# Stationary weight blocks laid out as element-wise mixed pairs and read with a step of two

## The chip, the cores and the metric

The kernel runs on one core of a Trainium2 chip. The metric is the device time of one execution in microseconds. Before the change the median of two timed runs is 977.47 us (976.68 and 978.26).

## What is computed

The reference is a two-layer decoder trunk for one sequence of 256 tokens and a model width of 1024, all in float32. Each layer has a feed-forward, a token mixer, and a second feed-forward; each of the three is preceded by an RMS norm that is shifted and scaled by vectors computed from a conditioning input `c`, and its result is added to the residual stream through a gate:

```
def swiglu(h, w_in, w_out):
    g, u = jnp.split(h @ w_in, 2, axis=-1)
    return (jax.nn.silu(g) * u) @ w_out

h = modulate(rms_norm(x, norm_g[layer, 0]), sh1, sc1)
x = x + 0.5 * g1[:, None, :] * swiglu(h, ffn_w_in[layer, 0], ffn_w_out[layer, 0])
h = modulate(rms_norm(x, norm_g[layer, 1]), sh2, sc2)
mix = diff_attention(...)        # layer 0; forgetting_attention(...) in layer 1
x = x + g2[:, None, :] * mix
h = modulate(rms_norm(x, norm_g[layer, 2]), sh3, sc3)
x = x + 0.5 * g3[:, None, :] * swiglu(h, ffn_w_in[layer, 1], ffn_w_out[layer, 1])
```

The hidden width of a feed-forward is 2816. The mixer of layer 0 is a differential attention of 8 heads, that of layer 1 a forgetting attention of 16 heads over one key and value pair that is computed once. Nearly all of the arithmetic is in products of the 256 tokens with weight matrices, and every weight is used once.

## The kernel before

**Precision.** A float32 product is made of three matmuls on operands in the type `fp32r`. A weight is split into a rounded high part `wh` (a copy on ScalarE) and a low part `wl` (raw minus high, on VectorE), and an activation likewise into `HH` and `HL` (or `hidh` and `hidl`). `mm3` then adds high times high, low times high and high times low into one bank of PSUM (line 405 on):

```
mm(ps, wh, xh, start=first, stop=False, skip_group_check=True)
mm(ps, wl, xh, start=False, stop=False, skip_group_check=True)
mm(ps, wh, xl, start=False, stop=last, skip_group_check=True)
```

The first operand of `mm` after the output is the stationary one: a block of 128 contraction rows (the partitions) by 128 output features, loaded into the array by a LDWEIGHTS; the second is the moving one, 256 tokens (258 where two columns with the shift vector ride along). A block is therefore loaded three times.

**The stream of weights.** All weights go through one stream in a fixed order (`stream`, line 230 on). An entry is a source in DRAM, its number of columns and a step, and it is cut into two or three pieces of at most 1024 columns (`pieces`). SyncE's queue fetches the pieces in order into `raw` tiles (six buffers), ScalarE makes `wh` (`cp_part`, six buffers) and VectorE makes `wl` (`sub_part`, five buffers) from each. `take` hands out the next entry and returns `blk(c, w)`, which gives the high and low views of the columns from `c` on, `w` wide:

```
def blk(c, w=P):
    o = c % step
    ...
    return his[p0 + c // step][:, o:o + w], los[p0 + c // step][:, o:o + w]
```

A product of weights by tokens asks for `w = 128`: the first feed-forward matrix (tiles `pf`, `pg` and `pu`, and `lg` and `lu` where it starts before the norm is known), the second (`po<-hidh` and `po<-hidl`, eleven blocks to an entry), the query and key projections (`lp`, `pqk`, `pk`, `lq`) and the output projections (`pw`). Where the output is wanted with tokens on the partitions, the weights are the moving operand: the value projections (`pv`, 512 columns) and the last feed-forward's second matrix (`po<-wh` and `po<-wl`, 256 columns, entries named `wlast`).

**Order of work.** The engines' programs are in the order in which the Python code issues instructions. A small planner (`InOrder`) keeps an estimated clock for each engine, with a cost that goes by the shape of an instruction's first operand (its output), and fills the gaps of ScalarE and VectorE with the splits of later pieces and with the blocks of the conditioning product (`ada_block`). `blk` also tells it when the first piece of an entry is done with.

**Layout.** `_layout` arranges every weight on the host as plain arrays, before the launch: `gu`, `kouter`, `bpairs`, and the lines for `wout` and `wqk` put the 128-column blocks that follow one another in use next to one another in memory.

Of the kernel before, what the change touches and what calls it, by code (L numbers as in the profile page):

```python
# [17 lines left out]
P = 128  # L18
D = 1024
S = 256  # L20
NC = D // P
HD = 64
AH = 8
# [80 lines left out]
def trunk(ctx, tc, a, out):  # L104
# [125 lines left out]
    stream = []  # L230
# [4 lines left out]
    def add_ffn(l, i):  # L235
        if (l, i) == (0, 0):
            stream.extend((a["win0"][k], K0 * 512, 1024) for k in range(NC))
        n = 2 * (NG - K0 if (l, i) == (0, 0) else NG)
        stream.extend((a["win"][win0_of(l, i) + u], 2048, 1024) for u in range(n))
        if (l, i) == (1, 1):  # L240
            for u in range(4):
                stream.extend((a["wlast"][u, :, c:c + n], n, step)
                              for c, n, step in ((0, 2048, 1024), (2048, 2048, 1024), (4096, 1536, 768)))
        else:
            stream.extend((a["wout"][(2 * l + i) * 16 + u], 11 * P, 768) for u in range(16))
# [11 lines left out]
    stream += [(a["wo"][u], 2048, 1024) for u in range(4, 8)]  # L257
    add_ffn(1, 1)

    pieces = [(src, c0, min(step, ncols - c0), c0 + step >= ncols)  # L260
              for src, ncols, step in stream for c0 in range(0, ncols, step)]

    shift = {}
    for (l, i), j in ((0, 0), K0), ((0, 1), 1), ((1, 0), 0), ((1, 1), 1):
# [7 lines left out]
    raws, his, los = [], [], []  # L272
# [20 lines left out]
    def cp_part():  # L293

        u = len(his)
        n = pieces[u][2]
        act.t = max(act.t, used[u - NHI] if u >= NHI else 0.0)
        raw = raws[u]
        if u >= len(pieces) - 6:
            gated[0](raw[:, :n])  # L300
        wh = wp.tile([P, WB], F32R, tag="wh", name="wh")[:, shift.get(u, 0):]
        act.plainly(lambda: act.copy(wh[:, :n], raw[:, :n]))
        his.append(wh)

    def sub_part():

        u = len(los)
        if u == len(his):
            return
        n = pieces[u][2]  # L310
        dve.t = max(dve.t, used[u - NLO] if u >= NLO else 0.0)
        wl = wp.tile([P, WB], F32R, tag="wl", name="wl", bufs=NLO)[:, shift.get(u, 0):]
        dve.plainly(lambda: dve.tensor_tensor(wl[:, :n], raws[u][:, :n], his[u][:, :n].bitcast(F32),
                                              op=ALU.subtract))
        los.append(wl)
        w_dma()
# [8 lines left out]
    def take(src, split=False):  # L325

        u = taken[0]
        assert stream[u][0].tensor.name.endswith(src), (stream[u][0].tensor.name, src)
        p0 = done[0] = begun[0]
        while len(used) < p0:  # L330
            used.append(pe.t)
        while len(his) < p0 + 2:
            cp_part()
        while len(los) < p0 + 2:
            sub_part()
        taken[0] += 1
        begun[0] += 2
        step = stream[u][2]

        def blk(c, w=P):  # L340
            o = c % step
            if c >= step and not split and done[0] == p0:
                done[0] = p0 + 1
                used.append(pe.t)
            return his[p0 + c // step][:, o:o + w], los[p0 + c // step][:, o:o + w]
        return blk

# [559 lines left out]
    for k in range(0, NC, 2):  # L907
# [3 lines left out]
        if k % 4:  # L911
            i = k // 4
# [461 lines left out]
def _constants():  # L1374
    idx = np.arange(383)
    rel = 255 - idx
    n = np.maximum(rel, 0)
    me = NB // 2
    nf = np.maximum(n, 1).astype(np.float32)
    large = me + (np.log(nf / np.float32(me)) / np.float32(math.log(128 / me)) * np.float32(NB - me)).astype(np.int32)  # L1380
    large = np.minimum(large, NB - 1)
    bucket = np.where(n < me, n, large)
    hot = np.zeros((NB, 383), np.float32)
    hot[bucket, idx] = 8.0
    umask = np.where(rel < 0, NEG, 0.0).astype(np.float32)
    q = np.arange(P)
    cmask = np.zeros((P, S), np.float32)
    cmask[:, P:] = np.where(q[:, None] >= q[None, :], 0.0, NEG)
    ub = np.full((P, S), 8.0, np.float32)
    ub[:, :P] = np.where(q[:, None] <= q[None, :], 8.0, 0.0)  # L1390
    return dict(hot=hot, umask=umask, cmask=cmask, ub=ub, ident=np.eye(P, dtype=np.float32))


def _layout(x, c, ada_w, ada_b, norm_g, ffn_w_in, ffn_w_out, a_w_qkv, a_w_o, a_lambda,
            a_subln_g, rel_bias, kv_ada_w, kv_ada_b, kv_norm_g, kv_w, fgate_w, fgate_b,
            b_w_q, b_w_o, final_g):
    cat = np.concatenate
    r = {}
    r["x"] = x[0].T.reshape(NC, P, S).transpose(1, 0, 2)
    r["c"] = c.reshape(1, D)  # L1400

    def cols(v):
        return v.reshape(-1, P).T

    def pairs(m):
        m = m.reshape(-1, P, D)
        return m

    ada, adab = [], []

    def unit(b0, b1, v0, v1):
        ada.append(cat([b0, b1], axis=1))
        adab.extend([v0, v1])

    def ada_sec(wT, bb, sec):
        return wT[sec * D:(sec + 1) * D].reshape(NC, P, D), bb[sec * D:(sec + 1) * D].reshape(NC, P)

    def mod_pair(wT, bb, s_sc, s_sh):
        w1, b1 = ada_sec(wT, bb, s_sc)
        w0, b0 = ada_sec(wT, bb, s_sh)  # L1420
        for j in range(NC):
            unit(w1[j], w0[j], b1[j], b0[j])

    for l in range(2):
        if l == 1:
            mod_pair(kv_ada_w.T, kv_ada_b, 1, 0)
        wT = ada_w[l].T
        for s in range(3):
            mod_pair(wT, ada_b[l], 3 * s + 1, 3 * s)
            w, b = ada_sec(wT, ada_b[l], 3 * s + 2)  # L1430
            for j in range(0, NC, 2):
                unit(w[j], w[j + 1], b[j], b[j + 1])
    r["ada"] = np.stack(ada)
    r["vecs"] = cat([cols(norm_g), cols(kv_norm_g), cols(final_g), cols(a_subln_g), np.stack(adab, axis=1)], axis=1)

    def gu(w):
        g = w[:, :FF].reshape(NC, P, NG, 256)
        u = w[:, FF:].reshape(NC, P, NG, 256)
        return cat([g, u], axis=3)

    win = []
    for l in range(2):
        for i in range(2):
            w = gu(ffn_w_in[l, i])
            if (l, i) == (0, 0):
                r["win0"] = w[:, :, :K0].reshape(NC, P, K0 * 512)
                w = w[:, :, K0:]
            n = w.shape[2]
            win.append(w.reshape(2, 4, P, n, 512).transpose(3, 0, 2, 1, 4).reshape(2 * n, P, 2048))
    r["win"] = cat(win, axis=0)  # L1450
    w = ffn_w_out.reshape(4, FF, D)
    r["wout"] = w[:3].reshape(3, 2, 11, P, NC, P).transpose(0, 4, 1, 3, 2, 5).reshape(48, P, 11 * P)
    r["wlast"] = w[3].reshape(22, P, 4, 256).transpose(2, 1, 0, 3).reshape(4, P, 22 * 256)
    r["fin"] = final_g.reshape(1, D)

    def vmat(w):
        return w.reshape(2, 4, P, 2, 512).transpose(3, 0, 2, 1, 4).reshape(4, P, 2048)

    def kouter(w):
        return w.reshape(4, 2, P, D).transpose(0, 2, 1, 3).reshape(4, P, 2048)  # L1460

    def bpairs(w):
        return w.reshape(NC, P, 4, 256).transpose(2, 1, 0, 3).reshape(4, P, 2048)

    w = a_w_qkv[0]
    qk = cat([w[:, :D].reshape(NC, P, AH, P), w[:, D:2 * D].reshape(NC, P, AH, P)], axis=3)
    r["wqk"] = qk.transpose(2, 1, 0, 3).reshape(AH, P, 2048)
    r["wv"] = vmat(w[:, 2 * D:])
    r["wo"] = cat([kouter(a_w_o[0]), kouter(b_w_o[0])], axis=0)
    r["wkk"] = bpairs(kv_w[:, :D])  # L1470
    r["wkv"] = vmat(kv_w[:, D:])
    r["wq"] = bpairs(b_w_q[0])
    r["fgw"] = fgate_w.reshape(NC, P, BH).transpose(1, 0, 2)
    r["fgb"] = fgate_b.reshape(BH, 1)
    k = _constants()

    def rows(v):
        return np.concatenate([v, np.zeros((P - v.shape[0], v.shape[1]), np.float32)], axis=0)

    r["misc"] = cat([k["ident"], k["cmask"], k["ub"], rows(k["hot"]),  # L1480
                     np.broadcast_to(k["umask"], (P, 383)), rows(rel_bias),
                     np.broadcast_to(a_lambda.reshape(1, 4 * HD), (P, 4 * HD))], axis=1)
    return {k: np.ascontiguousarray(v) for k, v in r.items()}
# [16 lines left out]
```

## Time and profile before

| | |
|---|---|
| median of two timed runs | 977.47 us |
| span of the profiled execution, first to last instruction | 974.4 us |
| TensorE matmuls | busy 963.7 us (99%), 8124 |
| TensorE weight loads | busy 939.9 us (96%), 8124 |
| VectorE | busy 818.5 us (84%) |
| ScalarE | busy 552.4 us (57%) |
| moved by DMA | 268.22 MB, mean 275 GB/s |

The page gives the span of the profiled execution and no separate total time for it. PE is the matmul side of TensorE and PEld its weight loads; DVE is VectorE, ACT ScalarE. Matmuls overlap one another in the records (each is listed with about 276 ns while one starts every 113 ns or so), so the listed durations of matmuls can't be added up; start times and counts within a stretch of the timeline can. L99 is the line of the helper that records nearly all instructions, so instructions are told apart by their tiles, written output<-inputs.

### The profile page before, as it was taken

To read this page: it belongs to the slowest core of one execution; us is meant where nothing else is said; L and a number is where in the kernel's file an instruction comes from. 1 tells how busy PE (TensorE), PEld (TensorE's weight loads), DVE (VectorE), ACT (ScalarE), POOL (GpSimd) and SP (SyncE) were. 2 spreads that over 40 slices of the span, in tenths; PEclk is the share of its full clock that TensorE was granted. 3 is DMA by queue.
4 is the path that set the end of the run, shared out by engine and by line. 5 is a ranking of instruction groups with operands and counts; after the bars stand their busy time and mean duration, and the time that the engine had idled before them with its cause. 6 is when DMAs were issued, how large, how long until landed. Compare 5 with 4: busy or idle time off the path is not lost.

```text
span 974.4 us, 20491 instructions
## 1 busy us (share of the span) xinstructions
PE 963.7 (99%) x8124; PEld 939.9 (96%) x8124; DVE 818.5 (84%) x1372; ACT 552.4 (57%) x902; POOL 54.6 (6%) x94
## 2 busy tenths in 40 slices
PE   8999999999999999999999999999999999999997
PEld 6999999998999999999997999999998999999997
DVE  7989979989999999878899989989977699555575
ACT  5466545566787645455576554445567576455432
POOL 0000200000112000000000000000011014300000
PEclk9999999999999999999999999999999999999999
DMA  9988999967776699888959899998885337978651
GB/s 360 415 352 279 332 372 339 345 225 272 293 239 232 209 381 370 293 287 314 329 179 370 308 338 337 345 314 319 297 278 174 104 109 228 266 149 276 185 152 44
DMA packets 69473, 268.22 MB, mean 275 GB/s; under 512 B 9417, under 2 KB 10225, under 8 KB 59266
## 3 DMA queue, kind: packets, MB, share of 16 engines
q1 hardware_dynamic: 66016, 259.69, 76.1%
q0 software_dynamic: 3072, 6.92, 2.5%
q8 instruction: 63, 1.03, 0.4%
q10 hardware_dynamic: 290, 0.32, 0.1%
q14 instruction: 32, 0.26, 0.1%
HBM read 264.75 MB, written 2.66 MB: 274 GB/s over the span
## 4 chain that ended last, share of the span: by engine, by line
PE 97%; DVE 1%; DMA 1%; ACT 0%; issue 0%; SPq 0%; DVEq 0%; ACTq 0%
PE po L99 25%; PE pg L99 21%; PE pu L99 21%; PE pf L99 5%; PE pv L99 5%; PE pw L99 4%; PE lp L99 4%; PE pqk L99 3%; PE wb L99 1%; PE lq L99 1%; PE lu L99 1%; PE lg L99 1%; PE pk L99 1%; PE sb L99 1%; DMA ada<-in_ada 1%; PE s L99 1%
## 5 line engine op out<-in xcount | busy, mean ns | idle before, releaser
L99 ACT CAST wh<-raw 128x1024 fp32r<-128x1024 f32 (+1 forms) x360 | 347.3, 975 | 210.8 <-PE pu L99 82.0
L99 DVE TENSOR_TENSOR wl<-raw,wh 128x1024 fp32r<-128x1024 f32 (+1 forms) x360 | 398.6, 1126 | 70.9 <-ACT sg L99 20.3
L99 DVE CUSTOM_DVE_ANT_0 ada<-ada,cact,vecs 128x1024 f32<-128x1024 f32 x160 | 203.6, 1279 | 0.4 <-DMA ada<-in_ada 0.4
L99 PE MATMUL pg<-HH,wh 128*128 128x256 f32 x608 | 168.0, 276 | 0.0
L99 PE MATMUL pg<-HH,wl 128*128 128x256 f32 x608 | 167.9, 276 | 0.0
L99 PE MATMUL pu<-HH,wh 128*128 128x256 f32 x608 | 167.9, 276 | 0.0
L99 PE MATMUL pu<-HL,wh 128*128 128x256 f32 x608 | 167.9, 276 | 0.0
L99 PE MATMUL pg<-HL,wh 128*128 128x256 f32 x608 | 167.9, 276 | 0.0
L99 PE MATMUL pu<-HH,wl 128*128 128x256 f32 x608 | 167.9, 276 | 0.0
L99 PE MATMUL po<-hidh,wh 128*128 128x256 f32 x528 | 145.7, 276 | 0.0
L99 PE MATMUL po<-hidh,wl 128*128 128x256 f32 x528 | 145.7, 276 | 0.0
L99 PE MATMUL po<-hidl,wh 128*128 128x256 f32 x528 | 145.7, 276 | 0.0
L99 PEld LDWEIGHTS pg<-HH,wh 128*128 128x128 f32 x608 | 114.1, 188 | 0.7 <-issue 0.6
L99 PEld LDWEIGHTS pg<-HH,wl 128*128 128x128 f32 x608 | 114.1, 188 | 0.0
L99 PEld LDWEIGHTS pu<-HH,wh 128*128 128x128 f32 x608 | 114.1, 188 | 0.0
L99 PEld LDWEIGHTS pg<-HL,wh 128*128 128x128 f32 x608 | 114.1, 188 | 0.0
L99 PEld LDWEIGHTS pu<-HL,wh 128*128 128x128 f32 x608 | 114.1, 188 | 0.0
L99 PEld LDWEIGHTS pu<-HH,wl 128*128 128x128 f32 x608 | 114.1, 188 | 0.0
L99 PEld LDWEIGHTS po<-hidh,wh 128*128 128x128 f32 x528 | 99.1, 188 | 0.0
L99 PEld LDWEIGHTS po<-hidl,wh 128*128 128x128 f32 x528 | 99.1, 188 | 0.0
L99 PEld LDWEIGHTS po<-hidh,wl 128*128 128x128 f32 x528 | 99.1, 188 | 0.0
L99 ACT CAST hidh<-hf 128x512 fp32r<-128x512 f32 x44 | 27.3, 621 | 40.5 <-DVE hf L99 40.4
(226 smaller groups left out, 1848.4 us busy)
## 6 DMA issues: line engine op xcount, KB each, us to landing
raw<-in_win SPq DMA_DIRECT2D x176, 512.0 KB, 6.8
ada<-in_ada SPq DMA_DIRECT2D x79, 1024.0 KB, 7.2
raw<-in_wout SPq DMA_DIRECT2D x48, 384.0 KB, 5.3
raw<-in_wout SPq DMA_DIRECT2D x48, 320.0 KB, 5.5
raw<-in_wqk SPq DMA_DIRECT2D x16, 512.0 KB, 5.8
raw<-in_wo SPq DMA_DIRECT2D x16, 512.0 KB, 5.8
raw<-in_wlast SPq DMA_DIRECT2D x16, 512.0 KB, 4.5
raw<-in_wv SPq DMA_DIRECT2D x8, 512.0 KB, 7.2
```

The source lines that it names most:

```text
L99: return self.tc.keep_in_program_order(f(*args, **kw))
```

## The change

The host writes the blocks of a pair (two neighbouring 128-column blocks, 256 columns) element by element in turn: first element of the first block, first element of the second, and so on (`mixed`). This is done for every weight that is used as a stationary operand. `blk`, asked for 128 columns, returns a view with a step of two elements that starts at the first or the second element of the pair. The pieces of `wout` hold eleven blocks to an entry, so that the last block of an entry has no partner; `mixed` leaves it as it is, and `blk` finds that the pair would reach past the piece (the fourth member of a stream entry gives a piece's width) and returns it as before. Views that are 256 or 512 wide are not touched.

```
+    stream = [(src, ncols, step, lambda i, n=ncols, s=step: min(s, n - i * s)) for src, ncols, step in stream]
     pieces = [(src, c0, min(step, ncols - c0), c0 + step >= ncols)
-              for src, ncols, step in stream for c0 in range(0, ncols, step)]
+              for src, ncols, step, _ in stream for c0 in range(0, ncols, step)]
...
+            if w == P:
+                o, n = o // 256 * 256, o // P % 2
+                if o + 256 <= stream[u][3](c // step):
+                    return tuple(t[p0 + c // step][:, o + n:o + 256:2] for t in (his, los))
+                o += n * P
             return his[p0 + c // step][:, o:o + w], los[p0 + c // step][:, o:o + w]
...
+    def mixed(w):
+        return np.swapaxes(w.reshape(w.shape[:-1] + (w.shape[-1] // 256, 2, P)), -1, -2).reshape(w.shape)
+
     def gu(w):
...
-        return cat([g, u], axis=3)
+        return mixed(cat([g, u], axis=3))
...
-    r["wout"] = w[:3].reshape(3, 2, 11, P, NC, P).transpose(0, 4, 1, 3, 2, 5).reshape(48, P, 11 * P)
+    w3 = w[:3].reshape(3, 2, 11, P, NC, P).transpose(0, 4, 1, 3, 2, 5).reshape(48, P, 11 * P)
+    r["wout"] = cat([mixed(w3[:, :, :10 * P]), w3[:, :, 10 * P:]], axis=2)
...
     def kouter(w):
-        return w.reshape(4, 2, P, D).transpose(0, 2, 1, 3).reshape(4, P, 2048)
+        return mixed(w.reshape(4, 2, P, D).transpose(0, 2, 1, 3).reshape(4, P, 2048))
...
     def bpairs(w):
-        return w.reshape(NC, P, 4, 256).transpose(2, 1, 0, 3).reshape(4, P, 2048)
+        return mixed(w.reshape(NC, P, 4, 256).transpose(2, 1, 0, 3).reshape(4, P, 2048))
...
-    r["wqk"] = qk.transpose(2, 1, 0, 3).reshape(AH, P, 2048)
+    r["wqk"] = mixed(qk.transpose(2, 1, 0, 3).reshape(AH, P, 2048))
```

## The prediction

> **What bounds the kernel now.** I read the page first: the share of each engine, the granted clock and the chain of work that ended last.
>
> ```profile
> span 974.4 us, 20491 instructions
> ...
> PE 963.7 (99%) x8124; PEld 939.9 (96%) x8124; DVE 818.5 (84%) x1372; ACT 552.4 (57%) x902; POOL 54.6 (6%) x94
> ...
> PEclk9999999999999999999999999999999999999999
> ...
> PE 97%; DVE 1%; DMA 1%; ACT 0%; issue 0%; SPq 0%; DVEq 0%; ACTq 0%
> ```
>
> TensorE is the bound in every stage: it carries 97% of the chain, and the granted clock is in its top step from the first slice to the last. Busy time says little for pipelined matmuls, so I went to start times. First the count per stretch (start:end, length, busy and number, clock, DMA share, GB/s), here 80 us inside the second feed-forward:
>
> ```profile
> 339.00:419.00 80.00, 80.00 (x708) 1.00 0.94 346
> ```
>
> Two of the 708 were already running when the stretch began, so 706 started in 80 us: one matmul each 113.3 ns. What makes up that interval is seen in the timeline of both TensorE queues (start, duration, engine, operation):
>
> ```profile
> 380.02 0.28 PE L99 MATMUL pg<-HL,wh 128*128 128x256 f32 x1
> 380.03 0.19 PEld L99 LDWEIGHTS pg<-HH,wh 128*128 128x128 f32 x1
> 380.14 0.28 PE L99 MATMUL pg<-HH,wh 128*128 128x256 f32 x1
> 380.14 0.19 PEld L99 LDWEIGHTS pg<-HH,wl 128*128 128x128 f32 x1
> ```
>
> A weight load starts at 380.03, about 0.01 us after the matmul before its own, and its matmul starts 0.11 us later, as the next load begins. So there is one load per matmul, and load and matmul fill the same 113 ns side by side. The change lengthens the kernel if the load becomes the slower of the two, and shortens it only if the load is what holds the matmul back now.
>
> How fast can contiguous loads follow each other? Where matmuls are short (128 columns of plain float32), the loads set the pace:
>
> ```profile
> 242.79 0.75 PEld L99 LDWEIGHTS po<-va,wt 128*128 128x128 f32 x6
> 243.46 0.19 PEld L99 LDWEIGHTS pqk<-HH,wh 128*128 128x128 f32 x1
> ```
>
> Six loads in 0.67 us are 111.7 ns each. Against 113.3 that leaves the load 1.6 ns of slack, 1.4%. That is the only cover the change has.
>
> And the moving side alone? The value projection streams 512 columns per load:
>
> ```profile
> 514.89 0.40 PE L99 MATMUL pv<-wh,HH 128*128 128x512 f32 x1
> ...
> 517.69 0.40 PE L99 MATMUL pv<-wh,HH 128*128 128x512 f32 x1
> ```
>
> Counting the rows between, twelve matmuls start in 2.80 us, 233.3 ns each. The second 256 columns come without a second load, and cost 233.3 - 113.3 = 120 ns, no less than the first. So I read the 113.3 ns as the pace of the moving stream, not as a cost of the load: a quicker load would find the matmul in its way.
>
> **The change part by part.** The host writes the weights in another order. The diff alters no size of a transfer, no tile, no number of instructions and no order: the planner's cost of a matmul goes by its output's shape, and the names it looks up are those of before. DMA, the two splits on ScalarE and VectorE, and every wait are as they were; they cost nothing more, and their cover (a TensorE that is the bound) stays unless TensorE itself gets faster. What changes is the read of the stationary block: 128 elements with a step of two, 8 bytes, spread over 1,024 bytes of a partition instead of 512.
>
> How many loads? The loads that read the low part, by tile (duration is min/median/max; the last number is the commonest form's count):
>
> ```profile
> L99 PEld LDWEIGHTS pg<-HH,wl x608: 187/188/191, 60.5 to 906.9; 128*128 128x128 f32 x152
> L99 PEld LDWEIGHTS pu<-HH,wl x608: 187/188/189, 61.3 to 907.5; 128*128 128x128 f32 x152
> L99 PEld LDWEIGHTS po<-hidh,wl x528: 187/188/188, 137.8 to 714.9; 128*128 128x128 f32 x176
> L99 PEld LDWEIGHTS po<-wl,hidh x176: 187/188/189, 907.9 to 967.5; 128*128 128x128 f32 x176
> L99 PEld LDWEIGHTS pf<-HH,wl x128: 186/188/192, 14.4 to 60.2; 128*128 128x128 f32 x128
> L99 PEld LDWEIGHTS lp<-HH,wl x96: 188/191/193, 197.6 to 726.9; 128*128 128x128 f32 x96
> L99 PEld LDWEIGHTS pqk<-HH,wl x96: 187/188/192, 234.1 to 277.6; 128*128 128x128 f32 x96
> L99 PEld LDWEIGHTS pv<-wl,HH x64: 187/188/192, 209.7 to 534.9; 128*128 128x128 f32 x64
> L99 PEld LDWEIGHTS pw<-oh,wl x64: 187/188/192, 277.9 to 306.1; 128*128 128x128 f32 x64
> L99 PEld LDWEIGHTS pw<-obh,wl x64: 187/188/192, 747.8 to 786.6; 128*128 128x128 f32 x64
> L99 PEld LDWEIGHTS lg<-HH,wl x32: 188/191/193, 306.4 to 797.9; 128*128 128x128 f32 x32
> L99 PEld LDWEIGHTS lu<-HH,wl x32: 189/190/192, 307.2 to 798.6; 128*128 128x128 f32 x32
> L99 PEld LDWEIGHTS pk<-HH,wl x32: 187/188/189, 499.3 to 509.8; 128*128 128x128 f32 x32
> L99 PEld LDWEIGHTS lq<-HH,wl x32: 187/191/193, 727.3 to 747.5; 128*128 128x128 f32 x32
> ```
>
> In two of these rows (po<-wl,hidh, the last down projection, and pv) the weights are the moving operand and stay contiguous. The other twelve sum to 608 + 608 + 528 + 128 + 96 + 96 + 64 + 64 + 4 x 32 = 2,320 blocks. mm3 loads each block three times (high, low, high): 6,960. Of the eleven blocks in half a column of the down projections the last has no partner and stays contiguous: 528/11 x 3 = 144. That leaves N = 6,816 loads with a step. Each nanosecond on the interval is 6.8 us, or 0.7% of the span; 2%, about what a measurement of this kernel can tell from no change, is 2.9 ns.
>
> The price of one stepped load is in no row, so I bound it. From below: the load keeps its 111.7 ns, hides behind the moving 113.3, and the sum is zero. Below zero: something in the pairing of load and matmul goes away. The shortest interval of a 128-column load that I find is in the transposes:
>
> ```profile
> 739.58 0.61 PE L99 MATMUL wa<-tri,d 128*128 128x128 f32 x4
> ...
> 740.02 0.38 PE L99 MATMUL wb<-tri,d 128*128 128x128 f32 x2
> ```
>
> Four in 0.44 us, 110 ns, or 109 within the rounding of the starts: (113.3 - 109) x 6,816 = 29 us less. From above, mildly: matmuls of the same shape (128 by 128 weights, 256 columns) run at other intervals elsewhere in this kernel, with contiguous loads.
>
> ```profile
> 53.73 0.28 PE L99 MATMUL pf<-HH,wh 128*128 128x256 f32 x1
> ...
> 54.79 0.28 PE L99 MATMUL pf<-HH,wh 128*128 128x256 f32 x1
> ```
>
> ```profile
> 510.40 0.28 PE L99 MATMUL pzf<-HH,fg 128*128 128x256 f32 x1
> ...
> 511.84 0.28 PE L99 MATMUL pzf<-HH,fg 128*128 128x256 f32 x1
> ```
>
> Nine matmuls in 1.06 us (117.8 ns), and twelve in 1.44 us (120 ns). From above, harshly: a stepped load at half rate, 2 x 111.7 = 223 ns.
>
> I take zero. The load delivers 128 elements in its 111.7 ns, 4 bytes each 0.87 ns; the moving stream takes 4 bytes each 0.44 ns from the same kind of memory. A load with a step of two passes over bytes at the moving stream's rate, 1,024 in about 113 ns, which that stream shows can be done. It is near the limit of 1.6 ns, though, and this is the weak point of the sum.
>
> The Trainium skill has a rule on just this (SBUF — State Buffer, section "Door 1: The DMA port swizzle", and Advanced Engine Details and Errata, "SBUF Cachelines"): lines are 16 bytes, and full bandwidth needs at least two hits on a line. A step of two float32 gives exactly two, so by the rule the load stays as it is and the sum is zero too; no run here shows a stepped load.
>
> The sum: 974.4 + 0 = 974.4 us of span. The page gives no other total for that execution; the median of the runs, 977.47, lies 3.1 us above the span, and I carry that over: 977.5 us. This case alone would land between 972 and 983.
>
> **The rivals.** *The stepped load is a little slower than the stream (slower).* If passing over twice the bytes costs the load a few per cent, its pace of 111.7 ns rises above the stream's, the load sets the interval, and matmuls wait for weights instead of for their own stream. It decides from 113.3 ns of load pace on, only 1.6 ns away; how far it goes I take from the intervals this kernel already shows, 117.8 to 120 ns. Priced by the two rows above: 4.5 x 6,816 = 31 us and 6.7 x 6,816 = 46 us, so 1,008 to 1,023 us. For it: in those rows loads and stream, both contiguous, already fall into a longer interval, and the step doubles the bytes that the load passes over. Against it: the feed-forward holds 113.3 over 706 matmuls beside full DMA traffic (share 0.94) and both splits.
>
> *The stepped load runs at half rate, or in between (much slower).* (223 - 113.3) x 6,816 = 748 us, 1,725 us. For it: nothing in the trace excludes it, since no load has a step. Against it: the moving stream's rate.
>
> *Load and stream stop disturbing each other (faster).* With the step both advance by the same bytes per time, and what separates 113.3 from 110 or 109 could go: 22 to 29 us, 948 to 955 us; if the load's 111.7 remains the floor, 1.6 x 6,816 = 11 us, 966 us, which is within 2%. Against it: the second 256 columns of pv cost 120 ns with no load beside them, and a gain of 4% meets a DMA share of 0.94 in the feed-forwards, so the last microseconds would turn into waits for weights.
> The Trainium skill (TensorE: Matmul & The Clock Gate, "Back-to-back issue gap") gives 262 cycles at 2.4 GHz for 256 columns, 109.2 ns, so 949 us if that were reached; the trace's 113.3 does not agree with it.
>
> *The change doesn't do what it says:* stepped reads could be turned into something else when the program is built. Then loads would change in number, which I fold into the harsh case.
>
> **How the numbers follow.** No change 0.41; mildly slower 0.27; harsh or in between 0.12; faster 0.20, of which a quarter stops at the load's floor. Beyond 2% faster (below 958): 0.15. Beyond 2% slower (above 997): 0.26 of the mild case and the 0.12, so 0.38. Within: 0.47. The range takes in 948 (the transposes' interval) and 1,030 (the mild case at 120 ns with a little more); left out are the harsh case and the edges, some 0.18.
>
> **What would show it.** Right: the feed-forward stretch again holds 113.3 ns per matmul, loads again start 0.01 us behind the matmul before, and the loads' forms keep their counts. The mild rival: the same stretch at 117 to 121 ns and the distance from load to matmul longer than 0.11 us, while pv and the last down projection, which keep contiguous reads, stay as they are. Faster: under 111 ns, and new idle time of TensorE on the high or low tiles. Wrong altogether: if stages without a stepped load moved, the cause is elsewhere.

## The result and the profile after

The changed kernel takes 1016.53 us (median of 1015.79 and 1017.28) against 977.47 us: 4.0% slower, ratio 1.0402 with a 95% interval from 1.0372 to 1.0432. The forecast case was "no change"; what came is the first rival of the prediction, a stepped load that is a little slower than the stream.

The page of the changed kernel, its lines on the span, the busy time, the granted clock and the chain of waits:

```profile
span 1013.7 us, 20491 instructions
...
PE 1003.9 (99%) x8124; PEld 981.3 (97%) x8124; DVE 821.9 (81%) x1372; ACT 554.5 (55%) x902; POOL 55.2 (5%) x94
...
PEclk9999999999999999999999999999999999999999
...
PE 97%; DVE 1%; DMA 1%; ACT 0%; issue 0%; SPq 0%; DVEq 0%; ACTq 0%
```

The span grew by 39.3 us and TensorE's busy time by 40.2 us. The number of instructions, the clock and the chain are those of before, and the work of the other engines nearly so: no wait was added, the matmuls themselves come at a longer interval. The count per stretch of the changed kernel, 80 us inside the second feed-forward (columns as in the prediction):

```profile
352.00:432.00 80.00, 80.00 (x669) 1.00 0.89 323
```

Two were already running, so 667 started in 80 us, one each 119.9 ns, where before 706 started. The timeline of both TensorE queues there:

```profile
352.19 0.28 PE L99 MATMUL pu<-HH,wl 128*128 128x256 f32 x1
352.19 0.20 PEld L99 LDWEIGHTS pu<-HL,wh 128*128 128x128 f32 x1
352.31 0.28 PE L99 MATMUL pu<-HL,wh 128*128 128x256 f32 x1
352.31 0.19 PEld L99 LDWEIGHTS pg<-HH,wh 128*128 128x128 f32 x1
```

The order is as before: a load starts with the matmul ahead of its own. But its matmul follows 0.12 us later instead of 0.11. The tiles of the changed kernel show which loads got longer (min/median/max in ns, first and last start in us):

```profile
L99 PEld LDWEIGHTS pg<-HH,wl x608: 193/193/199, 60.8 to 943.8; 128*128 128x128 f32 x152
...
L99 PEld LDWEIGHTS po<-hidh,wl x528: 187/193/199, 142.4 to 745.0; 128*128 128x128 f32 x176
...
L99 PEld LDWEIGHTS po<-wl,hidh x176: 187/188/189, 944.9 to 1006.8; 128*128 128x128 f32 x176
```

The stepped loads went from 187/188/191 to 193/193/199. The contiguous ones kept 187 to 189: those of the last down projection, and the eleventh blocks, which give `po<-hidh` its minimum of 187.

Where the time went, as the sum over all matmuls of a kind of the distance from one start to the next (worked out from the starts of both traces):

| tile | matmuls | before, us | after, us | gain in time |
|---|---|---|---|---|
| `pg`, `pu` | 3648 | 414.2 | 438.0 | 23.8 |
| `po`, down projections with stepped loads and small products | 1600 | 180.7 | 190.8 | 10.2 |
| `pqk`, `pw`, `pk` | 792 | 94.9 | 98.0 | 3.1 |
| `po`, last down projection, no stepped load | 528 | 59.9 | 62.1 | 2.2 |
| `pf`, `lp`, `lq`, `lg`, `lu`, all stepped | 960 | 117.9 | 117.7 | -0.2 |

These five rows hold 39.1 of the 39.3 us. Two of them fit neither the forecast nor the rival: a stage without a stepped load got slower, and a row of 960 stepped loads cost nothing in sum.

### The profile page after: what moved, and what is told of

Same layout as the page of the kernel before. It is cut to its first block, busy times and chain, and to the rows that moved or that the text cites. A ratio compares the mean times of both kernels' runs of the same rounds, so it can differ in the third digit from the quotient of the medians.

```text
span 1013.7 us, 20491 instructions
## 1 busy us (share of the span) xinstructions
PE 1003.9 (99%) x8124; PEld 981.3 (97%) x8124; DVE 821.9 (81%) x1372; ACT 554.5 (55%) x902; POOL 55.2 (5%) x94
## 4 chain that ended last, share of the span: by engine, by line
PE 97%; DVE 1%; DMA 1%; ACT 0%; issue 0%; SPq 0%; DVEq 0%; ACTq 0%
PE po L99 25%; PE pg L99 22%; PE pu L99 22%; PE pf L99 5%; PE pw L99 4%; PE pv L99 4%; PE pqk L99 3%; PE lp L99 3%; PE wb L99 1%; PE lq L99 1%; PE lg L99 1%; PE lu L99 1%; PE pk L99 1%; PE sb L99 1%; DMA ada<-in_ada 1%; PE s L99 1%
## 5 line engine op out<-in xcount | busy, mean ns | idle before, releaser
L99 PE MATMUL pu<-HH,wl 128*128 128x256 f32 x608 | 171.9, 283 | 0.0
L99 PE MATMUL pg<-HH,wl 128*128 128x256 f32 x608 | 171.9, 283 | 0.0
L99 PEld LDWEIGHTS pg<-HH,wh 128*128 128x128 f32 x608 | 118.1, 194 | 0.7 <-issue 0.6
L99 PEld LDWEIGHTS pg<-HL,wh 128*128 128x128 f32 x608 | 118.2, 194 | 0.0
L99 PEld LDWEIGHTS pu<-HL,wh 128*128 128x128 f32 x608 | 118.2, 194 | 0.0
L99 PEld LDWEIGHTS pu<-HH,wh 128*128 128x128 f32 x608 | 118.1, 194 | 0.0
L99 PEld LDWEIGHTS pg<-HH,wl 128*128 128x128 f32 x608 | 117.7, 194 | 0.0
L99 PEld LDWEIGHTS pu<-HH,wl 128*128 128x128 f32 x608 | 117.7, 194 | 0.0
L99 PEld LDWEIGHTS po<-hidl,wh 128*128 128x128 f32 x528 | 102.7, 195 | 0.0
L99 PE MATMUL po<-wl,hidh 128*128 128x256 f32 x176 | 49.5, 281 | 0.0
```

The costliest lines, as they stand in the source:

```text
L99: return self.tc.keep_in_program_order(f(*args, **kw))
```

## The experiments

Two theories stood after the result. *Slow load*: the stepped load by itself takes longer than the stream that covers it. *Interplay*: load and stream go together differently, and the load's own pace says little. All runs but one (e11) start from the kernel before, so their memory holds contiguous blocks and a step reads other columns. Without changes, the kernel before ran in 976.85, 981.17 and 981.24 us beside the three groups of runs (e1 to e4, e5 to e8, e9 to e11). These differ by more than some of the effects, so the argument goes by intervals of a stage, not by totals.

### e1: other loads stepped, the weights contiguous

```
-                        ts = slice(t * P, t * P + P)
+                        ts = slice(t, 2 * P, 2)
...
-                o = (k % 2) * 256 + t * P
+                o = slice((k % 2) * 256 + t, (k % 2) * 256 + 256, 2)
...
-            mm(po[:, 0:P], wt[:, 0:P], v0, start=True, stop=True)
-            mm(po[:, P:2 * P], wt[:, P:2 * P], v0, start=True, stop=False)
+            mm(po[:, 0:P], wt[:, 0:2 * P:2], v0, start=True, stop=True)
+            mm(po[:, P:2 * P], wt[:, 1:2 * P:2], v0, start=True, stop=False)
...
-            st[c] = [w0[:, j * P:j * P + P] for j in range(4)] + [w1[:, j * P:j * P + P] for j in range(2)]
+            st[c] = [w[:, b + j:b + 256:2] for w, b in ((w0, 0), (w0, 256), (w1, 0)) for j in range(2)]
```

> The kernel before, with the weight blocks contiguous; instead the loads that the change left alone are stepped by two: the token blocks in the value projections (pv, 512 moving columns) and in the last down projection (po<-wh, po<-wl, 256 moving columns), and the softmax blocks in the attention products (po<-va,wt with 128 and wb<-vb with 64 moving columns of plain float32). The tokens or keys of a block are then others than the product calls for; all work is done. Theory 'slow load': the stepped load itself takes longer whatever moves beside it. Then the light products go from 111.7 to about 118 ns a load, pv stays at 226 to 233 ns (the load ends long before the stream), po<-wh goes from 113.3 to 120. Rival 'contention': the load alone is as quick as before, and load and stream hinder each other while both read. Then the light products stay at 112, pv gets some 7 ns longer (236 to 240), po<-wh goes to 120. Both give some 981 us in all (528 x 6.7 ns = 3.5 us).

The best place to see a load by itself is `wb`, where a load goes with a matmul of only 64 columns, so that the loads set the pace. The timeline of the weight loads, first of the kernel before, then of e1:

```profile
743.59 0.97 PEld L99 LDWEIGHTS wb<-vb,wta 128*128 128x128 f32 x8 [0.33 <-issue]
744.48 0.53 PEld L99 LDWEIGHTS wb<-vb,wtb 128*128 128x128 f32 x4
```

```profile
745.83 1.02 PEld L99 LDWEIGHTS wb<-vb,wta 128*128 128x128 f32 x8 [0.33 <-issue]
746.77 0.55 PEld L99 LDWEIGHTS wb<-vb,wtb 128*128 128x128 f32 x4
```

Eight loads take 0.89 us contiguous and 0.94 us stepped: 111.3 and 117.5 ns each. And the last down projection, whose stationary token blocks are stepped in e1 (count per stretch, 915 to 960 us), first before and then in e1:

```profile
915.00:960.00 45.00, 45.00 (x399) 1.00 0.44 129
```

```profile
915.00:960.00 45.00, 45.00 (x377) 1.00 0.48 139
```

Less the two that were already running, 397 starts in 45 us are 113.3 ns and 375 are 120.0 ns. The prediction's stretch from 339 to 419 us, contiguous here, holds 113.3 ns as before (709 matmuls). `pv`, whose loads were stepped too, went from means of 229.0 and 230.6 ns in its two stages to 233.3 ns in both (by the starts of the traces): 3 to 4 ns more, which neither theory had (no change, or 236 to 240 ns). A load of about 118 ns ends long before a stream of 230, so this is a first sign that the load's own pace isn't the whole. So the step makes a load about 6 ns slower with other operands too, and this without any change in the layout of the weights.

### e2 and e9: steps of four and of three

```
+            if w == P:
+                p = p0 + c // step
+                b = min(o // (P * 4) * P * 4, pieces[p][2] - P * 4)
+                return tuple(t[p][:, b + o // P % 4:b + P * 4:4] for t in (his, los))
             return his[p0 + c // step][:, o:o + w], los[p0 + c // step][:, o:o + w]
```

(e9 has 3 in place of 4.)

> The kernel before, with the 128-column weight blocks read with a step of four elements (16 bytes), without the other layout, so the products use other columns than they call for; all work is done. It gives the law of the cost. If the step costs one fixed amount: 120 ns a matmul, about 1024 us. If it goes by the bytes passed over (6.7 ns for each 512 more, as from step one to two): 133 ns, 977 + 6960 x 20 ns = 1116 us. If each line of memory now serves one element and its reading time shows: a load of 213 ns or more and a matmul each 220 ns, 977 + 6960 x 107 ns = 1720 us. 'Slow load' and 'contention' do not differ here.

> The kernel before, with the weight blocks read with a step of three elements (other columns than called for; all work is done). With a step of four the interval was 233 ns, and 128 loaded elements then lie on 128 lines of 16 bytes: 1.82 ns a line. With a step of two they lie on 64 lines, 1.82 x 64 = 117 ns, near the 118 to 119 ns pace that was measured; contiguous on 32, 58 ns, so that the elements and not the lines set the 113. Theory 'a line each 1.82 ns': three elements of step touch 96 lines, 175 ns: an interval of 175 to 180 ns and 977 + 6960 x 62 to 67 ns = 1408 to 1443 us. Rival 'two hits or none' (a line with fewer than two elements costs a full access for each element): as with a step of four, 233 ns, about 1810 us.

Measured: 1810.08 us with a step of four and 1392.37 us with three. The timeline of matmuls in a feed-forward, e2 and then e9:

```profile
699.66 0.40 PE L99 MATMUL pu<-HL,wh 128*128 128x256 f32 x1
...
700.83 0.40 PE L99 MATMUL pg<-HH,wl 128*128 128x256 f32 x1
```

```profile
499.79 0.34 PE L99 MATMUL pu<-HH,wh 128*128 128x256 f32 x1
...
500.66 0.34 PE L99 MATMUL pu<-HL,wh 128*128 128x256 f32 x1
```

Both times five intervals lie between the two rows: 234 and 174 ns each. Counted in 16-byte lines (the width comes from the Trainium skill, SBUF — State Buffer, section "Door 1: The DMA port swizzle"), a load of 128 float32 touches 32 lines with step one, 64 with two, 96 with three and 128 with four. 174 / 96 = 1.81 ns and 234 / 128 = 1.83 ns: beyond step two the load costs about 1.82 ns for each line. In the last down projection, contiguous in both runs, the interval was 113.3 ns.

The 233 ns that e9's rival "two hits or none" expected of a step of three did not come, but that rival was worked out too roughly. With a step of three, every four elements lie on three lines, so 32 of the 96 lines hold two of them and 64 hold one. Take for a line of two what it costs at a step of two (118.9 / 64 = 1.86 ns, from e8 below) and for a line of one what it costs at a step of four (1.83 ns): 32 x 1.86 + 64 x 1.83 = 177 ns, near the 174 measured. So a line costs about the same whether one or two elements are taken from it, and that a line with a single hit is costly was not refuted. Nor do these runs tell lines from bytes: for steps of one to four the lines touched are the bytes passed over divided by 16, and 174 ns for 1,536 bytes and 234 ns for 2,048 are equally well 0.11 ns a byte. A step of more than four would separate the two; it was not run. The total of e9 lies below the 1408 to 1443 us expected, in part because the interval is 174 ns and not 175 to 180.

### e7 and e8: shorter streams, loads contiguous or stepped

```
-        mm(ps, wl, xh, start=False, stop=False, skip_group_check=True)
-        mm(ps, wh, xl, start=False, stop=last, skip_group_check=True)
+        mm(ps[:, :192], wl, xh[:, :192], start=False, stop=False, skip_group_check=True)
+        pe.t += (ps.shape[1] - 192) / 2350
+        mm(ps[:, :192], wh, xl[:, :192], start=False, stop=last, skip_group_check=True)
+        pe.t += (ps.shape[1] - 192) / 2350
```

(The line on `pe.t` keeps the planner's clock, and so the order, as it was. e8 also has e2's edit with 2 in place of 4.)

> The kernel before, contiguous, but the second and third matmul of each three stream 192 tokens instead of 256 (the low and cross terms of the last 64 tokens are left out). It gives the contiguous load's own pace beside the weights' type: if that is the 111.7 ns seen with short plain products, two of three intervals are 111 to 112 and the first 113, and the time is 977 - 4640 x 1.6 ns = 970 us. If the stream of 256 held everything and a load can be quicker still, below 965.

> As e7 (192 tokens in the second and third matmul of each three), with all weight blocks read with a step of two (other columns than called for). Theory 'slow load': the stepped load has a pace of about 118 ns of its own, which no shorter stream lowers: 117 to 119 ns in two of three, 1005 to 1012 us. Rival 'disturbed read': the 120 ns come from load and stream together, so that a stream a quarter shorter takes some of it away: 113 ns or below in two of three, 985 us or below.

Two of three streams are a quarter shorter, so the loads should show their own pace. The timeline of weight loads, e7 and then e8:

```profile
339.86 0.19 PEld L99 LDWEIGHTS pg<-HH,wl 128*128 128x128 f32 x1
...
340.88 0.19 PEld L99 LDWEIGHTS pg<-HH,wl 128*128 128x128 f32 x1
```

```profile
351.91 0.20 PEld L99 LDWEIGHTS pg<-HH,wh 128*128 128x128 f32 x1
...
352.98 0.20 PEld L99 LDWEIGHTS pg<-HH,wh 128*128 128x128 f32 x1
```

Nine intervals each: 1.02 us / 9 = 113.3 ns contiguous, 1.07 us / 9 = 118.9 ns stepped. Totals 972.74 and 1009.21 us. So a contiguous load of this kind has a pace of its own of 113.3 ns, not 111.7, and a stepped one 118.9 ns, 1.86 ns for each of its 64 lines. (The few us that e7 gained are no sign of 111.7: its feed-forwards stayed at 113.3 ns, while `lp`, which had 258 columns, went from 120.8 to 114.3 ns by the starts.) Of the 6.7 ns by which the interval grew in the changed kernel, the load's own pace would account for 5.6; e3 below shows that the load's pace isn't the whole of it.

### e4 and e6: shorter loads, contiguous or stepped

```
-        mm(ps, wl, xh, start=False, stop=False, skip_group_check=True)
-        mm(ps, wh, xl, start=False, stop=last, skip_group_check=True)
+        mm(ps[:64], wl[:, :64], xh, start=False, stop=False, skip_group_check=True)
+        mm(ps[:64], wh[:, :64], xl, start=False, stop=last, skip_group_check=True)
```

(In e6 these two loads take every second of a block's 128 columns, 64 in all; the first of the three stays contiguous. The low products of the other 64 output features are left out in both.)

> The kernel before, contiguous, but the second and third matmul of each three load 64 weight columns instead of 128 (the low and cross terms of the upper 64 features of a block are left out). The moving stream keeps its 256 columns. If the 113.3 ns are the pace of the stream, as the prediction read them: 113.3 ns stay and the time is 974 to 980 us. If the load of 128 columns holds the matmul back now: the two of three fall to 110 or below, 4640 x 3.5 ns = 16 us less or more, 961 us or below.

> As e4 (the second and third load of each three with 64 columns, the upper 64 features without their low and cross terms), but these 64-column loads are read with a step of two from a span of 128 columns (other columns than the product calls for); the first load is whole and contiguous. Theory 'slow load': what costs is the length of the stepped load; at 64 columns it is far shorter than the stream, so the intervals are those of e4, 113.3 or 117.8 by stage, and the time is 977 to 1005 us (e4: 988). Rival 'disturbed read': a stepped load hinders the stream whatever its length; then 120 ns everywhere, 1014 us or more.

The count per stretch in three stages, e4 and then e6:

```profile
160.00:190.00 30.00, 30.00 (x267) 1.00 0.93 340
345.00:385.00 40.00, 40.00 (x342) 1.00 0.97 376
560.00:600.00 40.00, 40.00 (x356) 1.00 0.94 345
```

```profile
160.00:190.00 30.00, 30.00 (x262) 1.00 0.92 330
345.00:385.00 40.00, 40.00 (x349) 1.00 1.00 390
560.00:600.00 40.00, 40.00 (x349) 1.00 0.92 333
```

Less two each, e4 has 113.2, 117.6 and 113.0 ns; by the starts of the trace these are stages at exactly 113.3 and 117.8 ns, held without a break over the stretches shown. Shorter loads never gave less than 113.3: the stream has that pace too. They even made whole stages slower, without any step, and the run took 988.08 us, which neither case had expected. e6 has 115.4, 115.3 and 115.3 ns (115.6 by the starts) in all three, and 987.57 us, which lies in the range given for 'slow load', but not by the intervals that it expected. A load of 64 elements with a step of two touches 32 lines, so at 1.82 ns for a line it would take 58 ns (an estimate from e2 and e9) and should not count at all. The load's pace alone does not explain either run.

### e3, e5 and e10: one stepped load in three, in 24, in six

e3, the low part alone:

```
+            if w == P:
+                p = p0 + c // step
+                b = min(o // 256 * 256, pieces[p][2] - 256)
+                return his[p][:, o:o + w], los[p][:, b + o // P % 2:b + 256:2]
```

e5, the low part of the first block of a piece (e10: of the first block of every pair):

```
+            if w == P and o == 0:
+                return his[p0 + c // step][:, o:o + w], los[p0 + c // step][:, 0:256:2]
```

> The kernel before, with only the low part's loads stepped by two (one load in three), without the other layout, so the low parts are those of other columns; all work is done. If the cost belongs to each stepped load: 2320 x 6.7 ns = 15.5 us, about 993 us, with 120 ns before the wl matmul and 113.3 before the two others. If it is a state into which the pair of load and stream falls and in which it stays: all three near 118 to 120, above 1005 us.

> The kernel before, with a step of two in one load of 24: the low part of the first block of each piece (320 loads); that low part is of other columns, all work is done. So far one stepped load in three made all three intervals 120 ns. Theory 'state': load and stream hold one of a few fixed intervals (113.3, 117.8, 120 ns) over whole stages, and a stepped load throws them out of the shortest; if they stay out, the whole feed-forwards run at 117.8 to 120 and the time is above 1000 us. Rival 'relaxation': a few matmuls after the stepped load the 113.3 is back; then the cost is 320 x 6.7 to 20 ns = 2 to 6 us, 979 to 984 us.

> The kernel before, with a step of two in the low part's load of every second block (one load in six, 1160 loads; other columns, all work is done). One in 24 cost some 20 ns for each stepped load, spread over the four matmuls behind it; one in three and three in three both ended at 120 ns. Theory 'each stepped load costs 20 ns until the matmuls behind it are all at 120': 20/6 = 3.4 ns on the mean, 116.7 ns, and 1160 x 20 ns = 23 us, about 1000 us. Rival 'a jump between one in 24 and one in three': the pair doesn't recover between, 119 to 120 ns and about 1015 us.

Measured: 1016.03, 981.88 and 995.14 us. The count per stretch in the second feed-forward, e3, e5 and e10:

```profile
352.00:432.00 80.00, 80.00 (x669) 1.00 0.88 323
```

```profile
339.00:419.00 80.00, 80.00 (x703) 1.00 0.93 343
```

```profile
352.00:432.00 80.00, 80.00 (x688) 1.00 0.89 329
```

e3 has the very count of the changed kernel, with a third of its stepped loads. What one of them costs: the starts are 667, 701 and 686, and at 113.3 ns they would fill 75.59, 79.45 and 77.75 us. The rest of the 80 us, shared among 667/3, 701/24 and 686/6 stepped loads, is about 20, 19 and 20 ns each (in e5 one start more or less in the stretch would move this by 4 ns). The starts of e5 show how, around one stepped load:

```profile
341.79 0.28 PE L99 MATMUL pg<-HH,wh 128*128 128x256 f32 x1
341.90 0.28 PE L99 MATMUL pg<-HH,wl 128*128 128x256 f32 x1
...
342.38 0.28 PE L99 MATMUL pg<-HL,wh 128*128 128x256 f32 x1
```

From the first row to the last are five intervals; to the nanosecond, in the trace, they are 115, 120, 122, 115 and 115, and then 113.3 again. They sum to 20 ns over five times 113.3. So a stray stepped load costs 20 ns, spread over the next few matmuls; at one in three the interval reaches 120.0 ns, and with all three stepped it stays there. That the longer interval lasts once it is entered fell with e5; that it relaxes within a few matmuls held, though one load cost 20 ns and not 6.7.

### e11: the changed kernel with a contiguous tail

```
-            if w == P:
+            if w == P and u < len(stream) - 13:
```

(In the changed kernel; the weights ahead of the last down projection still lie mixed, so the columns come in another order.)

> The changed kernel, with contiguous reads in the last piece pair (48 matmuls) of the last first-matrix, just ahead of the last down projection (the layout stays mixed, so these blocks are of other columns; all work is done). In the changed kernel the last down projection, which has no stepped load, ran at 117.8 ns instead of 113.3. If that is a state handed on from the stepped matmuls ahead: contiguous matmuls between let the pair fall back to 113.3, and the last down projection takes 59.9 us instead of 62.2, some 1013.5 us in all. If it comes of something else in the changed kernel: 117.8 stays.

The last down projection, 955 to 1000 us, in the changed kernel and then in e11:

```profile
955.00:1000.00 45.00, 45.00 (x384) 1.00 0.41 118
```

```profile
955.00:1000.00 45.00, 45.00 (x400) 1.00 0.40 118
```

382 starts are 117.8 ns, 398 are 113.1 (113.3 by the starts of the trace). The same instructions run at the one or the other pace, depending on what ran before them: with contiguous loads just ahead the stage is back at 113.3 ns. By the starts of e11, the 48 matmuls with contiguous reads of mixed blocks were themselves back at 113.3 ns a few matmuls after the last stepped load, so the order in memory costs nothing by itself. But stepped loads ahead do not always leave a longer interval. In the changed kernel and in e3 the last down projection follows a stage at 120.0 ns and stands at 117.8; in e2, e8 and e9 it follows stepped loads just as directly and stands at 113.3. The run took 1013.24 us, near the 1013.5 expected; single runs of one kernel differ by as much as the 2.2 us of this stage, so it is the interval that shows the effect and not the total.

## Why the prediction was wrong at its centre and right in its range

The measured 1016.53 us lie in the stated range, 948 to 1,030, because the range took in the mild rival, which had a chance of 0.27. The forecast itself, no change at 977.5 us, was 39 us too low.

*TensorE is the bound, nothing else moves.* Right. The chain holds 97% PE in both, and instructions, transfers and their order are the same.

*One load per matmul, side by side; the change lengthens the kernel if the load becomes the slower.* Right as a condition, and it is what happened; that the interval follows the load's pace alone is more than the runs show (see what stays open).

*"Against 113.3 that leaves the load 1.6 ns of slack."* Wrong. The 111.7 ns were read from `po<-va,wt`, plain float32 blocks beside short streams; in e7 the loads of weights run at 113.3 ns as soon as the stream is shorter. The slack was nil. *"So I read the 113.3 ns as the pace of the moving stream, not as a cost of the load"* was half right: e4 shows the stream's pace at 113.3, e7 the load's at 113.3 as well. Two equal limits look like one, and the test with `pv` could see only one of them.

*"I take zero."* This is the step that failed. It let a load with a step of two pass over bytes at the moving stream's rate, 1,024 in about 113 ns, and so hide. By e8 the stepped load takes 118.9 ns, 5.6 more than the 113.3 that cover it. As a rate the guess was near: e9 and e2 pass over 1,536 and 2,048 bytes in 174 and 234 ns, 0.11 ns a byte, about what the stream takes. But there was no slack for a price 5% higher, and by the prediction's own sum each nanosecond on the interval is 6.8 us.

The rule of the Trainium skill that two hits on a 16-byte line give full bandwidth (SBUF — State Buffer, "Door 1: The DMA port swizzle"; Advanced Engine Details and Errata, "SBUF Cachelines") was weighed for zero; the measurement differs from it. Two hits cost 118.9 against 113.3 ns, 5%. The 174 and 234 ns of steps three and four do not speak against the rule, since there most or all of the lines give a single element.

*The mild rival: matmuls wait for weights at 117 to 121 ns, 1,008 to 1,023 us.* Right in the distance from load to matmul and in the time, 1016.5 us, and in mechanism as far as the runs show it. Its sum, 6.7 ns x 6,816 = 46 us, has two errors that partly cancel. First, not all 6,816 loads stood at 113.3 before. Loads of the kernel before, at `lq`, whose stream is 258 columns:

```profile
741.82 0.19 PEld L99 LDWEIGHTS lq<-HL,wh 128*128 128x128 f32 x1
...
742.18 0.19 PEld L99 LDWEIGHTS lq<-HL,wh 128*128 128x128 f32 x1
```

Three intervals in 0.36 us, 120 ns already without a step. In the row of 960 matmuls in the table `lp`, `lq`, `lg` and `lu` had therefore nothing to lose. `pf` did get slower, from 115.8 to 120.0 ns on the mean (by the starts), but its stops between matmuls (intervals of 160 ns and more) shrank from 3.9 to 1.2 us in all; what they waited for was not traced. `pqk` and `pw` stood in part at 117.8 and lost less than 6.7 ns. Second, *"pv and the last down projection, which keep contiguous reads, stay as they are"*: `pv` did; the last down projection did not. By the prediction's own words that would put the cause elsewhere. e11 shows that it comes of the stepped loads ahead of it after all, worth 2.2 us. The rival took its upper price from the `pzf` row, which stood at 120 ns without any step; that the stepped kernel came out at this very 120.0 no run explains, and as a price it was in part luck.

*The harsh rival, half rate.* It did not come with a step of two; e2 shows it at four.

*The faster rival.* In no run did a stage with 256 columns for each load go below 113.3 ns. So the 109.2 ns worked out from the Trainium skill (TensorE: Matmul & The Clock Gate, "Back-to-back issue gap") agree with none of them.

**What stays open.** By pace alone e3 should give (118.9 + 2 x 113.3) / 3 = 115.2 ns; it gives 120.0. A single stepped load costs 20 ns although it is itself only 5.6 ns slower. Shorter loads put whole stages at 117.8 ns (e4). Load and stream settle into a few fixed intervals (113.3, 115.6, 117.8, 120.0), and how they do it, or which one a stage falls into, is not visible in the records. So it is shown that the step of the stationary read is the cause, and how far the load's own pace carries it; the rest of the way from load to interval is not shown. Whether the load's price goes by lines or by bytes is open too. Why the kernel before itself varied between 977 and 981 us was not traced either: a stage at 117.8 would fit, but those runs were not profiled. Mixing by units of two or four elements was not run.

## What to carry to other kernels

Keep the stationary operand contiguous along its columns: with one load for each matmul of 256 columns there was no cover for a slower one here, even with a step of only two elements (with 512 columns, as in `pv` of e1, a stepped load still cost 3 to 4 ns). Before calling an interval "the pace of X", shorten X alone and see whether it falls; two limits at the same value hide each other. And a price taken from the other operand may be near and still not near enough: measure the operand that changes, at a place of the kernel where nothing hides it.

## What the runs showed of the hardware

- A stationary load of 128 float32 columns took 113.3, 118.9, 174 and 234 ns with steps of one to four elements (e7, e8, e9, e2). From step two on that is 1.8 to 1.9 ns for each 16-byte line touched, or 0.11 to 0.12 ns for each byte passed over; these runs do not tell the two apart.
- A contiguous load of 128 columns and a stream of 256 have the same pace, 113.3 ns (e7, e4).
- One stepped load among contiguous ones costs about 20 ns over the next few matmuls (e5, e10); one in three is as dear as all three, 120.0 ns (e3).
- The same instructions can hold one of two intervals for a whole stage, 117.8 or 113.3 ns, depending on the loads ahead of them (the changed kernel and e11), over 62 us here; stepped loads ahead do not always leave the longer one (e2, e8, e9).
